# Reading a broadcast row back four steps later, and splitting the memory in the first four merged tiles

## Chip, cores and metric

The kernel runs on one core of a Trainium2 chip. The time is device microseconds of one execution. The engines are TensorE (PE, with its weight loads PEld), VectorE (DVE), ScalarE (ACT), GpSimd (POOL) and SyncE (SP), which here only issues DMAs. Each engine works through its own queue in order; engines wait for one another through semaphores.

## The reference

One layer of a hybrid decoder trunk on 512 rows of 1024 values, with 256 memory rows.

```python
h = rms_norm(x, norm_mix)
q_a, k_a, v_a, u_b, gate_b, gate_c, g_a, g_b = split(h @ w_in)
o_a = stick_breaking_attention(q_a, k_a, v_a)          # 8 heads of 64, causal
y_b = gate_b * causal_depthwise_conv(gate_c * u_b, conv_w)
merged = sigmoid(g_a) * (o_a @ w_branch_a) + sigmoid(g_b) * (y_b @ w_branch_b)
x = x + merged @ w_mix_out
m = rms_norm(mem, norm_mem_kv)                         # the memory: 256 x 1024
x = x + memory_cross_attention(rms_norm(x, norm_mem_q), m, w_mem_q, w_mem_kv, w_mem_o)
gate, up = split(rms_norm(x, norm_ffn) @ w_ffn_in)
x = x + (silu(gate) * up) @ w_ffn_out
return rms_norm(x, norm_final)
```

The attention's weight of key s for query t is sigmoid(z) times the product of (1 − sigmoid(z)) over the keys between them; it is computed as the exponential of sums of logarithms.

## The kernel before

Everything is held transposed: features on the 128 partitions, the 512 rows along the free axis, 8 tiles of 128 features. Every fp32 product is made of three matmuls on a high and a low part (names that end in `h` and `l`): ACT casts the high part, and DVE subtracts it to get the low part (`split`, L176 and L177 or L172 and L174). A weight tile is loaded by SP into `wr`, cast by ACT to `wh` (L149), and DVE makes `wl` (L150); there are four buffers of each. A projection (`project`, `gemm`) is 24 matmuls of 512 columns into one of two PSUM banks, which DVE then reads out (L294, L353, L372, L378, L387).

The first stage is a loop of 16 steps (L561), over four pairs of heads p and, for each, four blocks of 128 keys kt from 3 down to 0; step i has p = i // 4, so steps 9 and 13 are the same block kt = 2 of pairs 2 and 3. In a step PE computes the scores of the next block (`scores`, z at L445), adds the sums of logarithms to the scores of this one (`weights`, z at L488 and L491), and multiplies the weights of the block before with the values (`values`, o at L510). Projections from the list `fill` are put between them. Around the matmuls:

- `scores`: ACT and DVE make the logarithms `e`, POOL zeroes what lies above the diagonal (`causal`, L402, the select).
- `fails` (L460): ACT and DVE split `e` into `l`, which L491 multiplies in the next step.
- `weights` (L480): ACT takes the exponential `a` (L493), POOL applies the select to `a`, DVE multiplies and splits it into `ah` and `al` (L497, L498).
- `values`: after the last block of a pair, DVE adds the two halves `ot` (L519).

The memory's norm is prepared inside this loop. At steps 1, 3, 5 and 7 (`MEM_AT`) ACT squares a quarter of the memory; at step 9 (`MEAN_AT`) `mem_factors` (L536) makes the 256 factors 1/rms as `rm`, on 128 partitions x 2. POOL writes them to DRAM as one row `rmd` (L542) and reads the row back broadcast to all partitions as `rmb` (L544). `rm` scales the memory's values (`vm`, L670) and `rmb` its keys (`km`, L649), both much later.

The second stage (L618) makes the eight tiles of `merged`: two gates (a projection and its readout g, L353), two branch products br, their products and sum on DVE (L633, L634), and a split into `mh` and `ml`. After tile `SUMS_AT` = 1 POOL starts `weight_sums`, which loads pieces of the last weight matrix, adds them on POOL (`pre`, L595) and stores the sums; it goes on to the end of the stage. After tiles 0, 2, 4 and 6 `mem_split` loads two of the memory's eight feature tiles and splits them, with the gain, into `mgh` (ACT, L611) and `mgl` (DVE, L612). Those parts are read by the products `km` and `vm` that follow the stage. The loads of `mem_split` and those of the residual `x` (L705) share eight buffers (`xpool`); the parts take buffers of the pool `upool` (50 buffers), in the order in which the program asks for them.

A scheduler sets each engine's order from the program's order and the dependencies. `after(i, earlier)` (L105) adds a dependency that only orders instructions and makes nothing wait.

Of the kernel before, what the change touches and what calls it, by code (L numbers as in the profile page):

```python
# [8 lines left out]
F32 = mybir.dt.float32  # L9
# [4 lines left out]
P = 128  # L14
D = 1024
S = 512
KD = D // P
# [4 lines left out]
MEM = 256  # L22
# [6 lines left out]
EPS = 1e-6  # L29
MEM_AT = (1, 3, 5, 7)  # L30
MEAN_AT = 9
EARLY = 2
WARM = 8
FIRST = 4
# [9 lines left out]
def hybrid_layer(ctx: ExitStack, tc: tile.TileContext, xT_d, memT_d, mem_d, cols_d, wv_d, win_d,  # L44
                 wbr_d, wmix_d, wmq_d, wmk_d, wmv_d, wmo_d, wfi_d, wfo_d, gfin_d, out):
    nc = tc.nc

    cpool = ctx.enter_context(tc.tile_pool(name="cpool", bufs=1))
# [14 lines left out]
    def nm(s):  # L63
        count[0] += 1
        return f"{s}{count[0]}"

    def unit(s, cols=512):
        return upool.tile([P, cols], F32R, tag="u", name=nm(s), padded_shape=[P, 512])
# [34 lines left out]
    exps, casts, lead, lows, loads = [], [], [], [], []  # L103

    def after(i, earlier):  # L105
        for e in earlier:
            tc.add_manual_dep(i.ins, e.ins.name, mybir.DependencyInfo(
                mybir.DependencyClass.NoSync, mybir.DependencyReason.DATA), reason="order")
# [7 lines left out]
    def rstd_of(var, n, s, tables=()):  # L116

        def new(t):
            return tmp(t, n) if n > TT else spool.tile([P, n], F32, tag=t, name=nm(t))

        v, y, a = new("rv"), new("ry"), new("ra")
        r = cpool.tile([P, n], F32, tag=s, name=nm(s))
        after(nc.scalar.activation(y, var, AF.Ln, bias=eps_t), tables)
        nc.vector.tensor_scalar(out=v, in0=var, scalar1=EPS, scalar2=None, op0=ALU.add)
        exps.append(nc.scalar.activation(y, y, AF.Exp, scale=-0.5))
        nc.vector.tensor_tensor(out=a, in0=y, in1=y, op=ALU.mult)
        nc.vector.scalar_tensor_tensor(out=a, in0=a, scalar=-0.5, in1=v, op0=ALU.mult,
                                       op1=ALU.mult)
        nc.vector.scalar_tensor_tensor(out=r, in0=a, scalar=1.5, in1=y, op0=ALU.add, op1=ALU.mult)
        return r  # L130
# [171 lines left out]
    def settle_behind(*last):  # L302
        while urgent or behind:
            (urgent or behind).pop(0)(*last)
# [131 lines left out]
    def scores(p, kt):  # L436
        c0, n = span(kt)
        keys = slice(kt * P, (kt + 1) * P)
        zs[p, kt] = []
        for hs in heads_of(kt):  # L440
            bank = ztile("z")
            zs[p, kt].append(bank)
            for i, h in enumerate(hs):
                for part in range(2):
                    nc.tensor.matmul(bank[:, i * n:(i + 1) * n], ks[p][h][:, keys],  # L445
                                     qs[p][h][part][:, c0:], start=i + part == 0, stop=part == 1,
                                     skip_group_check=True)
        for hs, bank in zip(heads_of(kt), zs[p, kt]):
            w = len(hs) * n
            z = bank[:, :w]  # L450
            e = tmp("e")[:, :w]
            nc.scalar.activation(e, z, AF.Abs)
            nc.scalar.activation(e, e, AF.Exp, scale=-1.0)
            nc.scalar.activation(e, e, AF.Ln, bias=1.0)
            nc.vector.scalar_tensor_tensor(out=e, in0=z, scalar=0.0, in1=e, op0=ALU.max,
                                           op1=ALU.add)
            causal(by_head(e, n))
            urgent.append(lambda *last, e=e, hs=hs: fails(p, kt, hs, e, n, last))
# [21 lines left out]
    def weights(p, kt):  # L480
        c0, n = span(kt)
        av[p, kt] = {}
        for hs, bank in zip(heads_of(kt), zs[p, kt]):
            w = len(hs) * n
            z = bank[:, :w]
            if kt < TT - 1:
                for part in carried(p, kt, hs):
                    nc.tensor.matmul(by_head(z, n)[:, :, P:], neg1, part, start=False, stop=False,  # L488
                                     skip_group_check=True)
            for part in sp[p, kt, hs]:  # L490
                nc.tensor.matmul(z, negtri, part, start=False, stop=True, skip_group_check=True)  # L491
            a = tmp("a")[:, :w]
            exps.append(nc.scalar.activation(a, z, AF.Exp))  # L493
            causal(by_head(a, n))
            ah, al = unit("ah")[:, :w], unit("al")[:, :w]
            r = r0[:, kt:kt + 1]
            nc.vector.tensor_scalar(out=ah, in0=a, scalar1=r, scalar2=None, op0=ALU.mult)  # L497
            als.append(nc.vector.scalar_tensor_tensor(out=al, in0=a, scalar=r, in1=f(ah),  # L498
                                                      op0=ALU.mult, op1=ALU.subtract))
            for h in hs:  # L500
                av[p, kt][h] = part_of((ah, al), hs, (h,), n)
# [21 lines left out]
    def load_mem(k2, t):  # L523
        nc.sync.dma_start(t, memT_d[2 * k2 * P:(2 * k2 + 2) * P, :].rearrange("(j p) t -> p j t",
                                                                              p=P))
# [3 lines left out]
    def mem_square(i):  # L529

        h, t = divmod(i, MT)
        mk = f(unit("mk"))
        nc.sync.dma_start(mk, mem_d[t, :, h * 512:(h + 1) * 512])
        nc.scalar.activation(mk, mk, AF.Square, scale=D ** -0.5, accum_out=ms[:, i:i + 1])

    def mem_factors():  # L536

        var = spool.tile([P, MT], F32, tag="mv", name="mv", bufs=1)
        nc.vector.tensor_tensor(out=var, in0=ms[:, :MT], in1=ms[:, MT:], op=ALU.add)
        rm = rstd_of(var, MT, "rm")  # L540
        d = dpool.tile([1, MEM], F32, tag="rm", name="rmd")
        nc.gpsimd.dma_start(d.rearrange("o (t p) -> p (o t)", p=P), rm)  # L542
        rmb = cpool.tile([P, MEM], F32, tag="rmb", name="rmb")
        nc.gpsimd.dma_start(rmb, d.broadcast_to([P, MEM]))  # L544
        return rm, rmb

    fill = []
    for p in range(TT):
        if p + 1 < TT:
            fill += [(qk_part, p + 1, 0), (qk_part, p + 1, 1)]  # L550
        fill += [(conv, p, i) for i in range(3)]
    for m in range(EARLY):
        fill += [(gate, m, 0), (gate, m, 1)]
# [7 lines left out]
    for i in range(len(steps) + 1):  # L561
        if i in MEM_AT:
            mem_square(MEM_AT.index(i))
        if i == MEAN_AT:
            rm, rmb = mem_factors()
        some = []
        while fill and (i == len(steps) or len(some) < (2 if steps[i][1] == 1 else 1)):
            some.append(fill.pop(0))
        if i + 1 < len(steps):
            to = lambda: scores(*steps[i + 1])  # L570
            if len(some) == 1:
                midway.append(to)
            else:
                some.insert(len(some) // 2, (to,))
        for g, *args in some:
            g(*args)
        if i < len(steps):
            weights(*steps[i])
        if i > 0:
            values(*steps[i - 1])  # L580
        settle_behind(*exps[-1:], *joined[-1:])
# [22 lines left out]
    def mem_split(k2):  # L604
        mk = xpool.tile([P, 2, MEM], F32, tag="x", name=nm("mk"))
        load_mem(k2, mk)
        his, los = unit("mgh"), unit("mgl")
        for j in range(2):
            k = 2 * k2 + j
            hi, lo = (u[:, j * MEM:(j + 1) * MEM] for u in (his, los))  # L610
            nc.scalar.activation(hi, mk[:, j, :], AF.Copy, scale=g_kv[:, k:k + 1])  # L611
            nc.vector.scalar_tensor_tensor(out=lo, in0=mk[:, j, :], scalar=g_kv[:, k:k + 1],  # L612
                                           in1=f(hi), op0=ALU.mult, op1=ALU.subtract)
            mg.append((hi, lo))
# [3 lines left out]
    for m in range(KD):  # L618
        sig = []
        for j in range(2):  # L620
            if (m, j) not in gates:
                gate(m, j)
            t = gates.pop((m, j))
            sigmoid = nc.scalar.activation(t, t, AF.Sigmoid)
            after(sigmoid, exps[-2:])
            sig.append(t)
        w = load_w(wbr_d[m])
        for j in (1, 0):
            if m == 0 and j == 0:
                gate(EARLY, 0)  # L630
            ps = mmtile("br")
            gemm(ps, w, (oT, yb)[j], 4 * j)
            nc.vector.tensor_tensor(out=sig[j], in0=ps, in1=sig[j], op=ALU.mult)  # L633
        nc.vector.tensor_tensor(out=sig[0], in0=sig[0], in1=sig[1], op=ALU.add)  # L634
        if m < KD - 1:
            merged.append(split(sig[0], "m"))
        if m == SUMS_AT:
            weight_sums(range(SUMS_FIRST), merged[m][0])
        if m % 2 == 0:
            mem_split(m // 2)  # L640


    km = []
# [796 lines left out]
```

## Time and profile before

| what | value |
|---|---|
| median of 3 runs | 851.28 us (851.17 to 852.26) |
| profiled execution, its own time | 852.17 us |
| its span, first to last instruction | 850.3 us |
| mean granted clock of TensorE | 0.993 |
| DMA moved | 143.73 MB, mean 169 GB/s |

Where the stages lie in the profiled execution, by the rows in order of time: the 16 steps until about 199 us, the merged tiles until 308.7 us, the memory's keys until 332 us, then its values, the residual products, the attention over the memory, and the FFN with the end. The rows below are read as: start in us, length in us, engine, line, operation, tile written <- tiles read, shape, count; in brackets at the end the idle time of that engine just before, and what ended it. A row of a stretch of several instructions has their count and their total length.

### The profile page before, as it was taken

How to read it: one execution, taken by the hardware profiler on the slowest of the kernel's cores; microseconds unless marked ns; L12 is line 12 of the kernel's file. 1: busy time of each engine (PE TensorE's matmuls, PEld its weight loads, DVE VectorE, ACT ScalarE, POOL GpSimd, SP SyncE). 2: the span in 40 equal slices, each digit the busy share in tenths (PEclk: the TensorE clock that was granted, in tenths of full speed). 3: DMA queues.
4: the chain of work that ended last, by engine and by line, in shares of the span. 5: the costliest groups of instructions: out<-in, count | busy, mean ns of one | idle time of the engine just before them, and what ended most of it. 6: DMA issues, size and time to landing. Idle time of an engine off the chain costs nothing.

```text
span 850.3 us, 12669 instructions
## 1 busy us (share of the span) xinstructions
PE 837.4 (98%) x4763; PEld 737.8 (87%) x4763; DVE 657.2 (77%) x1049; ACT 459.4 (54%) x818; POOL 158.0 (19%) x165
## 2 busy tenths in 40 slices
PE   9999998999999999999999999999999999999996
PEld 7888886888888889888888889999999999988885
DVE  8869978896766686578555688888888888899886
ACT  7567866575333254534444565655555555666654
POOL 0011121210466650065000010211111110000401
PEclk9999998999999999999999999999999999999998
DMA  8453453225587765566341324776776773465552
GB/s 298 154 162 104 137 89 82 92 74 173 210 309 292 287 250 184 175 244 234 131 122 50 91 71 141 189 189 176 183 188 176 192 191 91 144 222 204 176 184 99
DMA packets 51360, 143.73 MB, mean 169 GB/s; under 512 B 5762, under 2 KB 7042, under 8 KB 48483
## 3 DMA queue, kind: packets, MB, share of 16 engines
q1 hardware_dynamic: 41650, 107.89, 38.1%
q0 software_dynamic: 9360, 34.75, 15.7%
q8 instruction: 37, 0.61, 0.3%
q10 hardware_dynamic: 288, 0.28, 0.1%
q14 instruction: 25, 0.20, 0.1%
HBM read 125.20 MB, written 13.64 MB: 163 GB/s over the span
## 4 chain that ended last, share of the span: by engine, by line
PE 93%; DVE 4%; DMA 1%; ACT 1%; issue 0%; POOL 0%; DVEq 0%; POOLq 0%
PE z L864 15%; PE p L1133 12%; PE y L864 7%; PE pr L154 6%; PE pr L155 6%; PE pr L156 6%; PE v L864 4%; PE r L155 3%; PE r L154 3%; PE r L156 3%; PE v L272 3%; PE mq L156 2%; PE mq L154 2%; PE mq L155 2%; PE br L154 2%; PE br L155 2%
## 5 line engine op out<-in xcount | busy, mean ns | idle before, releaser
L149 ACT CAST wh<-wr 128x1024 fp32r<-128x1024 f32 x84 | 88.0, 1052 | 151.3 <-issue 67.1
L150 DVE TENSOR_TENSOR wl<-wr,wh 128x1024 fp32r<-128x1024 f32 x84 | 111.1, 1325 | 38.0 <-ACT wh L149 37.8
L154 PE MATMUL pr<-xgh,wh 128*128 128x512 f32 x288 | 113.8, 395 | 0.0
L155 PE MATMUL pr<-xgl,wh 128*128 128x512 f32 x288 | 113.3, 393 | 0.0
L156 PE MATMUL pr<-xgh,wl 128*128 128x512 f32 x288 | 112.9, 392 | 0.0
L595 POOL TENSOR_TENSOR pre<-pre 128x512 f32<-128x512 f32 x44 | 72.5, 1652 | 30.1 <-DMA pre<-in_w_ffn_out_dram 27.8
L833 POOL DMA_DIRECT2D ws<-in_w_ffn_in_dram x22 | 26.6, 1209 | 255.7 <-DVE wf L854 122.8
L864 PE MATMUL z<-xdh,wf 128*128 128x256 f32 x352 | 70.4, 283 | 0.0
L156 PEld LDWEIGHTS pr<-xgh,wl 128*128 128x128 f32 x288 | 54.6, 190 | 11.8
L154 PEld LDWEIGHTS pr<-xgh,wh 128*128 128x128 f32 x288 | 54.7, 190 | 10.9
L155 PEld LDWEIGHTS pr<-xgl,wh 128*128 128x128 f32 x288 | 54.7, 190 | 10.5
L885 ACT COPY sa<-z 128x256 f32<-128x256 f32 x44 | 16.4, 373 | 80.9 <-PE z L864 80.9
L864 PEld LDWEIGHTS z<-xdh,wf 128*128 128x128 f32 x352 | 58.0, 192 | 0.0
L854 DVE TENSOR_TENSOR wf<-s,wf 128x512 fp32r<-128x512 f32 x44 | 30.4, 691 | 25.7 <-ACT wf L853 25.3
L864 PE MATMUL z<-xdl,wf 128*128 128x256 f32 x176 | 49.8, 283 | 0.0
L945 DVE TENSOR_TENSOR wl<-wr,wh 128x1024 fp32r<-128x1024 f32 x33 | 41.0, 1242 | 3.7 <-ACT wh L1012 3.6
L1012 ACT CAST wh<-wr 128x1024 fp32r<-128x1024 f32 x33 | 34.6, 1049 | 4.2 <-DMA wr<-sums 1.9
L864 PE MATMUL y<-xch,wf 128*128 128x256 f32 x176 | 35.4, 283 | 0.0
L864 PE MATMUL v<-xoh,wf 128*128 128x256 f32 x176 | 35.4, 283 | 0.0
L864 PE MATMUL z<-xf,wf 128*128 128x256 f32 x264 | 35.4, 283 | 0.0
L864 PE MATMUL z<-xch,wf 128*128 128x256 f32 x176 | 35.3, 283 | 0.0
L864 PE MATMUL y<-xoh,wf 128*128 128x256 f32 x176 | 35.3, 283 | 0.0
(348 smaller groups left out, 2399.6 us busy)
## 6 DMA issues: line engine op xcount, KB each, us to landing
wr<-in_w_in_dram SPq DMA_DIRECT2D x36, 512.0 KB, 3.4
pre<-in_w_ffn_out_dram POOLq DMA_DIRECT2D x11, 1024.0 KB, 7.7
sums<-pre POOLq DMA_DIRECT2D x11, 1024.0 KB, 5.0
ws<-in_w_ffn_in_dram SPq DMA_DIRECT2D x22, 512.0 KB, 3.7
wg<-in_w_ffn_in_dram SPq DMA_DIRECT2D x22, 512.0 KB, 4.5
ws<-in_w_ffn_in_dram POOLq DMA_DIRECT2D x22, 512.0 KB, 6.0
wr<-sums SPq DMA_DIRECT2D x22, 512.0 KB, 4.0
wr<-in_w_ffn_out_dram SPq DMA_DIRECT2D x16, 512.0 KB, 3.8
```

Source lines behind the costliest of these rows:

```text
L149: after(nc.scalar.copy(h2, raw), lead[-1:])
L150: lows.append(nc.vector.tensor_tensor(out=l2, in0=raw, in1=f(h2), op=ALU.subtract))
L154: nc.tensor.matmul(ps, a[0], b[0], start=start, stop=False, **kw)
L155: nc.tensor.matmul(ps, a[0], b[1], start=False, stop=False, **kw)
L156: nc.tensor.matmul(ps, a[1], b[0], start=False, stop=stop, **kw)
L595: nc.gpsimd.tensor_tensor(out=t[:, a, :], in0=t[:, a, :], in1=t[:, b, :], op=ALU.add)
L833: nc.gpsimd.dma_start(s13, a[:, 0:4:3, :], accum_op=ALU.add)
L854: nc.vector.tensor_tensor(out=w[:, 1, :], in0=raw, in1=f(w[:, 0, :]), op=ALU.subtract)
L864: nc.tensor.matmul(ps[:, :HS], a, b, start=i < 3 and k == 0 and j == 0, stop=k == KP - 1 and j == 2, skip_group_check=True)
L945: nc.vector.tensor_tensor(out=lo, in0=src, in1=f(hi), op=ALU.subtract)
L1012: nc.scalar.copy(hi, raw)
L1133: nc.tensor.matmul(res[i][s2], a[:, ts], b, start=j == 0 and n == 0, stop=n == 2 and j == (BEHIND - 1 if (i, s2) == (5, 1) else NJ - 1))
```

## The change

It has two parts. The read-back of the row is taken out of `mem_factors`, which now returns the DRAM row, and is issued at step 13 (`ROW_AT`), ordered behind the last exponential that was issued by then, that of step 12. And `mem_split` is called after the merged tiles 0, 1, 2 and 3 in place of 0, 2, 4 and 6.

```diff
+ROW_AT = 13
...
-        rmb = cpool.tile([P, MEM], F32, tag="rmb", name="rmb")
-        nc.gpsimd.dma_start(rmb, d.broadcast_to([P, MEM]))
-        return rm, rmb
+        return rm, d
...
         if i == MEAN_AT:
-            rm, rmb = mem_factors()
+            rm, rmd = mem_factors()
+        if i == ROW_AT:
+            rmb = cpool.tile([P, MEM], F32, tag="rmb", name="rmb")
+            after(nc.gpsimd.dma_start(rmb, rmd.broadcast_to([P, MEM])), exps[-1:])
...
-        if m % 2 == 0:
-            mem_split(m // 2)
+        if m < KD // 2:
+            mem_split(m)
```

In the rows that follow, the number behind a name tells its buffers apart, and the lines of the changed kernel are one to three higher.

POOL around step 9, before: `a_1336` is the `a` of step 8's weights, `e_1314` the `e` of step 9.

```order
L402 AFFINE_SELECT a_1263<-a_1263 128x128
L542 DMA rmd<-rm_1380 128x2x1
L402 AFFINE_SELECT e_1314<-e_1314 128x2x128
L544 DMA rmb<-rmd 128x256
L402 AFFINE_SELECT a_1336<-a_1336 128x256
L402 AFFINE_SELECT a_1446<-a_1446 128x2x128
```

The same place in the changed kernel:

```order
L403 AFFINE_SELECT a_1263<-a_1263 128x128
L543 DMA rmd<-rm_1380 128x2x1
L403 AFFINE_SELECT e_1314<-e_1314 128x2x128
L403 AFFINE_SELECT a_1336<-a_1336 128x256
L403 AFFINE_SELECT a_1444<-a_1444 128x2x128
```

The select of `a_1336` now follows that of `e_1314` at once; the write `rmd` has kept its place. Four steps later POOL has, in the changed kernel (`a_1727` is the `a` of step 12, `e_1702` the `e` of step 13):

```order
L403 AFFINE_SELECT a_1663<-a_1663 128x128
L403 AFFINE_SELECT e_1702<-e_1702 128x2x128
L567 DMA rmb<-rmd 128x256
L403 AFFINE_SELECT a_1727<-a_1727 128x256
L403 AFFINE_SELECT a_1819<-a_1819 128x2x128
```

Before, these four selects stood there without the read between them. The other engines' order in the 16 steps is the same in both kernels.

DVE in merged tiles 6 and 7, before: `ml_2788` is the low part of merged tile 6, `mgl_2794` the memory's last parts, `g_2830` and `g_2864` the gates of tile 7.

```order
L150 TENSOR_TENSOR wl_2905<-wr_2902,wh_2904 128x1024
L353 TENSOR_TENSOR g_2830<-pr_2805,r0b_363 128x512
L150 TENSOR_TENSOR wl_2946<-wr_2943,wh_2945 128x1024
L174 TENSOR_TENSOR ml_2788<-g_2715,mh_2787 128x512
L612 SCALAR_TENSOR_TENSOR mgl_2794<-mk_2791,gcol,mgh_2793 128x256 x2
L353 TENSOR_TENSOR g_2864<-pr_2839,r0b_363 128x512
L150 TENSOR_TENSOR wl_2981<-wr_2978,wh_2980 128x1024
```

And in the changed kernel, where `ml_2689` is the low part of merged tile 5 and `ml_2796` that of tile 6:

```order
L151 TENSOR_TENSOR wl_2905<-wr_2902,wh_2904 128x1024
L354 TENSOR_TENSOR g_2830<-pr_2805,r0b_363 128x512
L151 TENSOR_TENSOR wl_2946<-wr_2943,wh_2945 128x1024
L175 TENSOR_TENSOR ml_2689<-g_2616,mh_2688 128x512
L175 TENSOR_TENSOR ml_2796<-g_2723,mh_2795 128x512
L354 TENSOR_TENSOR g_2864<-pr_2839,r0b_363 128x512
L151 TENSOR_TENSOR wl_2981<-wr_2978,wh_2980 128x1024
```

The two splits `mgl` are gone from this place, and tile 5's `ml`, which stood ahead of tile 6's gates before, stands here. The memory's parts have taken two buffers earlier, and tile 5's parts now get buffers that PE has to free first: its cast `mh` waits for PE, which it did not before. ACT's casts are moved in the same way.

DVE after merged tile 3, in the changed kernel (`ml_2467` is the low part of tile 3; `g_2509` is the next tile's first gate):

```order
L636 TENSOR_TENSOR g_2394<-g_2394,g_2428 128x512
L151 TENSOR_TENSOR wl_2588<-wr_2585,wh_2587 128x1024
L175 TENSOR_TENSOR ml_2467<-g_2394,mh_2466 128x512
L614 SCALAR_TENSOR_TENSOR mgl_2473<-mk_2470,gcol,mgh_2472 128x256 x2
L354 TENSOR_TENSOR g_2509<-pr_2484,r0b_363 128x512
L151 TENSOR_TENSOR wl_2622<-wr_2619,wh_2621 128x1024
```

Before, `ml` was followed there by the gate's readout at once; the same holds for tile 1. PE's order is the same in both kernels. On SP the loads of `x` for the residual's tiles 5 to 7, which need the buffers of the memory's tiles, move ahead with the splits, and one weight load goes behind the third memory load.

## The prediction

> **What bounds the kernel now.** I read the page first, then TensorE's waits, then order of time around the one long wait.
>
> ```profile
> PE 837.4 (98%) x4763; PEld 737.8 (87%) x4763; DVE 657.2 (77%) x1049; ACT 459.4 (54%) x818; POOL 158.0 (19%) x165
> PEclk9999998999999999999999999999999999999998
> PE z L491 <- DVE l L417: 4.0, 1, 4.0
> PE br L154 <- DVE g L353: 0.4, 1, 0.4
> ```
>
> TensorE (PE) is busy for 837.4 of 850.3 us, so it is the bound nearly everywhere, and a change pays only where PE stands still or runs slowly. The waits (total us, times, longest) leave two such places inside the kernel: one of 4.0 us, one of 0.4 us. The clock row (40 slices of 21.3 us) has an 8 in the seventh slice, 127.5 to 148.8 us, and one in the last.
>
> ```profile
> 128.51 0.39 PE L491 MATMUL z<-l,negtri 128*128 128x512 f32 x1
> 132.92 0.79 PE L491 MATMUL z<-l,negtri 128*128 128x512 f32 x1 [4.03 <-DVE l L417]
> 134.26 0.73 PE L154 MATMUL pr<-xgh,wh 128*128 128x512 f32 x1
> 139.30 0.40 PE L154 MATMUL pr<-xgh,wh 128*128 128x512 f32 x1
> 171.28 0.62 PE L491 MATMUL z<-l,negtri 128*128 128x512 f32 x2
> 172.13 0.44 PE L154 MATMUL pr<-xgh,wh 128*128 128x512 f32 x1
> 174.94 0.39 PE L154 MATMUL pr<-xgh,wh 128*128 128x512 f32 x1
> 128.51:132.92 4.41, 0.39 (x3) 0.07 (x2) 2.75 (x6) 0.74 (x2) 0.99 (x2) 0.92 0.60 142
> 132.92:139.30 6.38, 6.38 (x17) 5.18 (x18) 5.76 (x11) 5.89 (x12) 1.25 (x3) 0.52 0.28 64
> ```
>
> These are PE's rows in order of time in step 9 (first four) and step 13 (next three), and two rows of windows (length, then busy time of PE, PEld, DVE, ACT, POOL, the granted clock, DMA). Steps 9 and 13 are the same stretch of code for head pairs 2 and 3: two `z` matmuls of line 491, four short ones, then projections `pr`. In step 9 the second L491 waits 4.03 us, and the clock granted afterwards is 0.52 until 139.30. From the first L491 to the 13th `pr` matmul (both ends shown) step 9 takes 139.30 − 128.51 = 10.79 us, step 13 takes 174.94 − 171.28 = 3.66 us, at full clock without a wait. So this place loses **7.13 us**: 4.03 of waiting, and 3.10 because the matmuls behind it run at half clock.
>
> ```profile
> 119.72 0.73 POOL L542 DMA_DIRECT2D rmd<-rm  x1 [3.62 <-DVE rm L129]
> 121.07 0.40 POOL L402 TENSOR_SCALAR_AFFINE_SELECT e<-e 128x256 f32<-128x256 f32 x1 [0.62 <-DVE e L455]
> 129.04 0.57 POOL L544 DMA_DIRECT2D rmb<-rmd  x1 [7.57 <-DMA rmd<-rm]
> 129.63 0.42 POOL L402 TENSOR_SCALAR_AFFINE_SELECT a<-a 128x256 f32<-128x256 f32 x1
> 121.81 0.39 ACT L493 ACTIVATE a<-z 128x256 f32<-128x256 f32 x1
> 121.95 1.23 DVE L150 TENSOR_TENSOR wl<-wr,wh 128x1024 fp32r<-128x1024 f32 x1 [0.17 <-ACT wh L149]
> 130.08 0.35 DVE L497 TENSOR_SCALAR ah<-a,r 128x256 fp32r<-128x256 f32 x1 [6.91 <-POOL a L402]
> 132.17 0.69 DVE L417 TENSOR_TENSOR l<-e,l 128x512 fp32r<-128x512 f32 x1
> ```
>
> Who made `l` late: POOL's read-back `rmb` stands in its queue ahead of the select of `a`, and waits 7.57 us for the write of `rmd` to land. `a` was ready at 121.81 + 0.39 = 122.20, but its select starts at 129.63. DVE is in order: `ah` waits for the select, and behind `ah` are queued `ot`, `al`, `ot` and then `l`, for which PE waits.
>
> **The change, first part: the read moves four steps on.** Nothing is added or removed; one DMA issue moves past 12 POOL instructions. Without it the select runs at 122.2 to 122.7; DVE is at `wl` until 121.95 + 1.23 = 123.18, so `ah` starts at 123.2 instead of 130.08, 6.88 us earlier. With the same sequence behind it, `l` ends at 132.86 − 6.88 = 126.0; PE wants it one matmul (0.23) after 128.51, at 128.74. So the whole wait goes, with 2.7 us to spare. Step 13 has the same margin in the trace:
>
> ```profile
> 165.03 0.51 POOL L402 TENSOR_SCALAR_AFFINE_SELECT a<-a 128x256 f32<-128x256 f32 x1 [0.73 <-ACT a L493]
> 166.54 0.34 DVE L497 TENSOR_SCALAR ah<-a,r 128x256 fp32r<-128x256 f32 x1
> 168.63 0.69 DVE L417 TENSOR_TENSOR l<-e,l 128x512 fp32r<-128x512 f32 x1
> 139.78 1.21 DVE L150 TENSOR_TENSOR wl<-wr,wh 128x1024 fp32r<-128x1024 f32 x1
> 143.39 0.39 PE L156 MATMUL pr<-xgh,wl 128*128 128x512 f32 x1
> 134.00:200.00 66.00, 66.00 (x301) 55.48 (x301) 58.08 (x95) 45.99 (x83) 11.13 (x21) 0.96 0.30 99
> rmd<-rm POOLq DMA_DIRECT2D x1, 1.0 KB, 9.0
> rmb<-rmd POOLq DMA_DIRECT2D x1, 128.0 KB, 4.1
> L649 DVE TENSOR_TENSOR km<-km,rmb x8: 420/426/426, 311.8 to 331.9; 128x256 f32<-128x256 f32 x8
> ```
>
> There `l` ends at 168.63 + 0.69 = 169.32. The second L491 of the pair shown at 171.28 (0.62 for two, 0.39 for one) starts 0.23 later, at 171.51: 2.2 us of margin. The moved read now stands just ahead of this select of `a`, where POOL sits idle for 0.73 us; its issue took 0.57, so I price it at 0. At its worst it is as long as the longest select of this kernel, 1.8 us, and makes `a` 1.1 us late; but `a` ends 1.0 us before DVE comes to it, and behind that lie the 2.2 us. PE waits only if POOL is held for over 0.73 + 1.0 + 2.2, about 4 us. The write, issued at 119.72, landed 9.04 later at 128.76; the read now comes at about 164.3 − 7.1 = 157.2, 28 us after it, so the only wait that the read has is over. Its own 4.1 us are hidden, since `rmb` is first used at 311.8.
>
> What is late next, with the wait gone? DVE comes 6.88 us earlier, PE 7.13, so PE gets 0.25 us closer to DVE. The nearest product it uses is `wl`, which ends at 140.99 and is first used at 143.39: 2.40 us, still 2.15. SP's queue needs `qk` results that DVE and ACT now make about 7 us earlier.
>
> The clock row in that window counts as a term of its own. The Trainium skill, "TensorE: Matmul & The Clock Gate", section "What's actually happening", says that an idle window of about 3.4 us halves the clock and that such windows run on freely, whatever the kernel does. By that rule a pause of 4.03 us need not close the gate in every execution, and the gain would then be the wait alone. The trace agrees in this execution (0.52 after the pause); that it holds in the timed ones no row shows.
>
> Value taken for the first part: 7.13 us (ends: 4.03, no clock loss in the timed runs, and 7.13; nothing in the step is lost beyond what step 13 lacks).
>
> **Second part: the memory's splits after the first four merged tiles.** Four pairs of ACT copies `mgh` and four pairs of DVE splits `mgl` stay; those of m=4 and m=6 move to m=1 and m=3. Their loads stay at 192 to 195 us (row below), but for one weight load that goes behind the third of them, 0.45 us. Because two more buffers are taken early, the split `ml` of merged tile 5 slides behind tile 7's first gate.
>
> ```profile
> L524 SPq DMA_DIRECT2D mk<-in_memT_dram x4: 378/452/1029, 192.3 to 194.8; - x4
> 300.12 1.77 DVE L174 TENSOR_TENSOR ml<-g,mh 128x512 fp32r<-128x512 f32 x1
> 301.82 3.37 DVE L612 SCALAR_TENSOR_TENSOR mgl<-mk,gcol,mgh 128x256 fp32r<-128x256 f32 x2
> 305.11 0.68 DVE L353 TENSOR_TENSOR g<-pr,r0b 128x512 f32<-128x512 f32 x1
> 305.84 0.50 PE L154 MATMUL br<-oh,wh 128*128 128x512 f32 x1 [0.37 <-DVE g L353]
> 213.38 0.87 DVE L612 SCALAR_TENSOR_TENSOR mgl<-mk,gcol,mgh 128x256 fp32r<-128x256 f32 x2
> 221.19 0.69 DVE L353 TENSOR_TENSOR g<-pr,r0b 128x512 f32<-128x512 f32 x1 [2.29 <-PE pr L156]
> 248.39 0.69 DVE L353 TENSOR_TENSOR g<-pr,r0b 128x512 f32<-128x512 f32 x1 [2.29 <-PE pr L156]
> 248.21 1.05 ACT L149 CAST wh<-wr 128x1024 fp32r<-128x1024 f32 x1 [3.18 <-PE pr L155]
> 250.54 0.33 SPq L141 DMA_DIRECT2D wr<-in_w_branch_dram  x1
> ```
>
> At the end of the stage `ml` and two `mgl` took 1.77 + 3.37 = 5.14 us ahead of `g`; now two `ml` stand there, 2 × 1.77 = 3.54 at the same slow pace. `g` comes 1.6 us earlier and PE's 0.37 us go. More can't be won here: PE waits nowhere else in this stage. At m=1 and m=3 DVE idles 2.29 us before the next `g`, and the undisturbed pair costs 0.87; ACT idles 3.18 us (m=3), and its pair is 0.9. So 0. Its other end: if POOL's additions run at that moment, the pair is 3.37 us and `ml` 1.77, the load that cost 0.37 at 305; twice, 0.74. The fourth late load of `x` now waits on SP for m=3's split, ahead of the weights issued at 250.54. That split ends 0.87 into the idle time that begins at 248.39 − 2.29, so at 247.0: 3.5 us of room. I take −0.37, with ends −0.37 and +0.37.
>
> **Sum.** Against the profiled execution's 852.17 us (span 850.3, 1.87 around it): 852.17 − 7.13 − 0.37 = **844.67**. The median of the runs shown is 851.28, 0.89 lower; the same 7.50 off it gives 843.78. The highest run, 852.26, equals the profiled one, so profiling as such adds little. I take 844.5, nearer to the sum in which every term was seen; 0.2% is 1.7 us, about what a measurement can tell from no change.
>
> **Rivals.**
>
> - The clock doesn't fall in the timed runs, so only 4.03 + 0.37 = 4.40 is won: 851.28 − 4.40 = 846.9. For it: one trace shows one execution. Against it: a run without the half clock would be 3.10 under the profiled 852.17, at 849.1, and the lowest is 851.17. This is what the free-running window in the Trainium skill, "TensorE: Matmul & The Clock Gate", section "What's actually happening", would do. Chance 0.10.
> - DVE becomes what PE waits for. DVE is busy 58.08 of the 66 us behind the place, so it can't follow much faster; if it eats the 3.10 that the full clock gives, 852.17 − 4.40 = 847.8. Against it: 2.15 us of margin at the nearest use, and step 13 runs at full clock with the same load. Chance 0.09.
> - The wait re-forms with nothing won, because the select of `a` was held by something else besides the read. `a` was ready at 122.20 and POOL idle from 121.47, so there is no sign of it: 850.9 to 851.3. Chance 0.04.
> - Slower: the read holds POOL in step 13. If its issue had to wait for a transfer as long as the write's 9.0 us plus its own 4.1, POOL would be held 13.7 us, less the idle 0.73 and the 3.2 us of margin: PE waits 9.7 us, and with 3.10 for the clock the time is 844.7 + 12.8 = 857.5. It decides from 4 us on (PE waits) and makes the kernel slower than before by over 0.2% from about 10 us. Against it: its one wait is for a write 28 us old. Chance 0.03.
>
> **How the numbers follow.** The forecast has 0.74, with a range of its own of 843.3 (median less 7.50, and half a microsecond of spread) to 846.0 (the profiled sum, 0.74 if both new places collide, and as much spread). The range for 8 in 10 reaches on to the two middle rivals, 847.8. Faster by over 0.2%: 0.74 + 0.10 + 0.09 = 0.93; within 0.2%: 0.04; slower: 0.03.
>
> **What would show it.** Right: no wait of PE on L491 near 129 us; clock 9 in the seventh slice; the `ah` of 130.08 near 123.2; `rmb` issued near 157 us (164.3 less 7) between two selects and the `a` behind it not late; no wait of `br` on `g`. The gaps of PE sum to about 7 us less, and the span is near 842.8. Wrong: a PE wait of over 0.5 us between 126 and 200, a half clock that stays, DVE splits at m=1 or m=3 of over 2 us followed by a PE wait, or a weight load on SP delayed behind an `x` load.

## The result, and the profile after

| | before | changed |
|---|---|---|
| median of 6 runs | 851.75 us (851.17 to 852.47) | 844.59 us (844.14 to 844.98) |
| span of the profiled execution | 850.3 us | 842.4 us |
| mean granted clock of TensorE | 0.993 | 0.998 |

The changed kernel takes 0.9915 of the time before, with a 95% interval of 0.9902 to 0.9928: 7.16 us less. The page of the changed kernel, with the busy times and the clock row (40 slices, now of 21.1 us):

```profile
PE 833.9 (99%) x4763; PEld 735.5 (87%) x4763; DVE 653.5 (78%) x1049; ACT 459.0 (54%) x818; POOL 152.8 (18%) x165
PEclk9999999999999999999999999999999999999999
```

The 8 in the seventh slice is gone, and PE's busy time falls by 3.5 us although it has as many matmuls: the slow ones ran at half clock. PE's waits in the changed kernel, the whole answer (us in total, times, longest):

```profile
PE warm L233 <- DVE neg L92: 1.4, 1, 1.4
```

Only the wait at the very start is left. The rows of the changed kernel in order of time around step 9 (its lines are one to three higher than before):

```profile
119.67 0.73 POOL L543 DMA_DIRECT2D rmd<-rm  x1 [3.62 <-DVE rm L130]
122.21 1.18 POOL L403 TENSOR_SCALAR_AFFINE_SELECT a<-a 128x256 f32<-128x256 f32 x1 [0.78 <-ACT a L494]
123.42 0.35 DVE L498 TENSOR_SCALAR ah<-a,r 128x256 fp32r<-128x256 f32 x1 [0.30 <-POOL a L403]
125.52 0.69 DVE L418 TENSOR_TENSOR l<-e,l 128x512 fp32r<-128x512 f32 x1
128.46 0.62 PE L492 MATMUL z<-l,negtri 128*128 128x512 f32 x2
132.12 0.39 PE L155 MATMUL pr<-xgh,wh 128*128 128x512 f32 x1
```

The write of the row is issued as before, but the select of `a` behind it no longer waits; `ah` starts at 123.42 in place of 130.08. `l` ends at 126.21, PE wants it at 128.46 + 0.23 = 128.69, so the two L492 run as one piece. The last row is the 13th `pr`: the stretch that took 10.79 us takes 132.12 − 128.46 = 3.66, to the hundredth what step 13 took before.

A better measure of a stage than the span is the distance between two matmuls of PE, since it leaves out the start of the kernel, which varies by about a microsecond. For step 9 I take the first `z` of the next two blocks' scores. Before:

```profile
124.80 0.87 PE L445 MATMUL z<-qk,qk 128*128 128x384 f32 x4
142.03 1.07 PE L445 MATMUL z<-qk,qk 128*128 128x512 f32 x4
```

And after:

```profile
124.76 0.87 PE L446 MATMUL z<-qk,qk 128*128 128x384 f32 x4
134.84 1.07 PE L446 MATMUL z<-qk,qk 128*128 128x512 f32 x4
```

That is 142.03 − 124.80 = 17.23 before and 10.08 after, 7.15 us. The same for other stretches, in every kernel that was profiled (each one execution):

| kernel | step 9 | step 11 | step 13 | first br to first km |
|---|---|---|---|---|
| before | 17.23 | 7.93 | 10.08 | 109.46 |
| before, second execution | 16.92 | 7.93 | 10.09 | 108.80 |
| changed | 10.08 | 7.92 | 10.08 | 108.80 |
| read alone | 10.08 | 7.93 | 10.08 | 108.82 |
| splits alone | 17.28 | 7.92 | 10.08 | 108.80 |
| read one select later | 10.08 | 7.93 | 10.08 | 108.80 |
| write and read in step 13 | 10.08 | 7.92 | 15.85 | 108.80 |
| POOL held in step 13 | 10.08 | 7.93 | 10.09 | 108.80 |
| fill with 17 | 14.51 | 9.55 | 10.08 | 108.82 |
| fill with 17, order held | 14.41 | 9.42 | 10.08 | 109.56 |
| fill with 13 | 14.31 | 9.54 | 10.08 | 108.80 |
| fill with 9 | 15.97 | 7.93 | 10.08 | 108.80 |
| fill with 4 | 17.24 | 7.93 | 10.09 | 108.80 |

(Step 9, 11 and 13: from the first `z` of the scores of steps 10, 12 and 14 to that of the next step; us.) The table answers most of what follows: a number away from its column's usual one is a place where PE stood still or ran slowly.

### The profile page after: what moved, and what is told of

The parts are those of the page before. It is cut to its first block, busy times and chain, and to the rows that moved or that the text cites. A ratio compares the mean times of both kernels' runs of the same rounds, so it can differ in the third digit from the quotient of the medians.

```text
span 842.4 us, 12670 instructions
## 1 busy us (share of the span) xinstructions
PE 833.9 (99%) x4763; PEld 735.5 (87%) x4763; DVE 653.5 (78%) x1049; ACT 459.0 (54%) x818; POOL 152.8 (18%) x165
## 4 chain that ended last, share of the span: by engine, by line
PE 99%; DVE 0%; ACT 0%; DVEq 0%; issue 0%
PE z L866 15%; PE p L1135 12%; PE pr L155 8%; PE pr L156 8%; PE pr L157 8%; PE y L866 8%; PE v L866 4%; PE r L156 3%; PE r L155 3%; PE r L157 3%; PE v L273 3%; PE mq L157 2%; PE mq L155 2%; PE mq L156 2%; PE br L157 2%; PE br L156 2%
```

## Experiments

### The two parts alone

Theory A is the prediction's: the read's wait costs 7.13 us, the splits 0.37, apart from each other. First the read alone, the splits as before:

```diff
-        if m < KD // 2:
-            mem_split(m)
+        if m % 2 == 0:
+            mem_split(m // 2)
```

> The kernel before with only the read of the row moved to step 13; the memory's splits stay at merged tiles 0, 2, 4 and 6. Theory A (the read's wait costs 7.13 us, the splits 0.37, independent of each other): 7.13 us under the kernel before, so about 844.6 beside 851.75, PE's wait on L491 gone, its 0.37 us wait of br on g still there. Rival B (the two parts help each other, or the splits carry more of the gain than the trace of before shows): 846 or more.

Measured: 844.40 us beside 850.90, ratio 0.9922 (0.9908 to 0.9935). That is the whole gain of the change, within the intervals (6.50 us here and not 7.13, which is taken up under "Span and time"). But PE's wait of `br` on `g`, which theory A left in place, is gone too. The read alone, DVE in order of time at the end of the merged stage:

```profile
290.84 1.23 DVE L151 TENSOR_TENSOR wl<-wr,wh 128x1024 fp32r<-128x1024 f32 x1 [0.21 <-ACT wh L150]
291.99 1.78 DVE L175 TENSOR_TENSOR ml<-g,mh 128x512 fp32r<-128x512 f32 x1
293.69 3.37 DVE L614 SCALAR_TENSOR_TENSOR mgl<-mk,gcol,mgh 128x256 fp32r<-128x256 f32 x2
296.98 0.68 DVE L354 TENSOR_TENSOR g<-pr,r0b 128x512 f32<-128x512 f32 x1
```

And the same `wl` in the kernel before:

```profile
298.25 1.94 DVE L150 TENSOR_TENSOR wl<-wr,wh 128x1024 fp32r<-128x1024 f32 x1 [0.21 <-ACT wh L149]
```

`ml` and the two `mgl` take as long as before, so the difference isn't in them. The `wl` ahead of them took 1.94 before and 1.23 here. That 0.71 decides, since PE waited 0.37 there.

Then the splits alone, on the kernel before:

```diff
-        if m % 2 == 0:
-            mem_split(m // 2)
+        if m < KD // 2:
+            mem_split(m)
```

> The kernel before with only the memory's splits moved to merged tiles 0 to 3; the read stays in step 9. Theory A: 0.37 us under the kernel before, about 851.4, within what a timing can tell from no change; PE's wait on L491 of 4.0 us and the half clock behind it stay, br's wait on g goes. Rival B: 850 or less.

Measured: 851.21 us beside 850.90, ratio 1.0000 (0.9991 to 1.0009). Its waits of PE show the 4.0 us, and no `br`:

```profile
PE z L491 <- DVE l L417: 4.0, 1, 4.0
PE warm L232 <- DVE neg L91: 1.4, 1, 1.4
```

So the splits alone gain nothing that a timing can tell. A second execution of the kernel before says why:

> The kernel before, unchanged, in a second profiled execution. If PE's 0.37 us wait of br on g at the end of the merged stage belongs to the kernel's order, it is there again and the stage from the first br to the first km takes 109.46 us again; if it was an accident of that one execution, the stage takes 108.80, as in the fill with 4, and the second part of the change has nothing to win. PE's wait of 4.0 us on L491 stays; the half clock behind it lasts 6.8 us if its length is fixed, 3.4 or 6.8 if it goes in whole windows that start anywhere.

Measured in this one run: 850.99 us, a wait of 3.84 us on L491, and 6.83 us of half clock behind it. In it `wl` and its neighbours read as follows:

```profile
297.62 1.23 DVE L150 TENSOR_TENSOR wl<-wr,wh 128x1024 fp32r<-128x1024 f32 x1 [0.21 <-ACT wh L149]
300.47 3.38 DVE L612 SCALAR_TENSOR_TENSOR mgl<-mk,gcol,mgh 128x256 fp32r<-128x256 f32 x2
```

`wl` takes 1.23, and PE doesn't wait for `g`: the merged stage takes 108.80, with the splits at their old place. Over all thirteen executions this `wl` took 1.22 to 2.17 us. Of the eight with the splits at the old place, the two in which it took 1.94 and 2.05 have the wait (109.46 and 109.56 in the table), and the six with 1.23 to 1.62 don't. With the new place there is no wait in five, not even where `wl` took the longest. The kernel of the next section (its splits at the new place), DVE and PE:

```profile
291.65 2.17 DVE L151 TENSOR_TENSOR wl<-wr,wh 128x1024 fp32r<-128x1024 f32 x1 [0.21 <-ACT wh L150]
297.14 0.68 DVE L354 TENSOR_TENSOR g<-pr,r0b 128x512 f32<-128x512 f32 x1
298.70 0.39 PE L155 MATMUL br<-oh,wh 128*128 128x512 f32 x1
```

`g` ends 0.88 ahead of `br` here, although `wl` took 0.94 longer than in the read alone, where `g` ends at 297.66 for a `br` at 297.90, 0.24 ahead. So the second part gives `g` 0.88 + 0.94 − 0.24 = 1.58 us more room, and takes away a wait that comes in some executions and costs about 0.7 us when it comes. Where it comes, the merged stage loses more than the 0.37 us that the wait is listed with: 109.46 − 108.80 = 0.66.

### Does the distance count, or only the one select?

The read is put back to step 9, one POOL instruction behind its old place:

```diff
-ROW_AT = 13
+ROW_AT = 9
...
-            causal(by_head(a, n))
+            selects.append(causal(by_head(a, n)))
...
-            after(nc.gpsimd.dma_start(rmb, rmd.broadcast_to([P, MEM])), exps[-1:])
+            after(nc.gpsimd.dma_start(rmb, rmd.broadcast_to([P, MEM])), selects[-1:])
```

> The changed kernel with the read put back to step 9, but behind the select of a instead of ahead of it: one POOL instruction later, not four steps. Theory A (only the select held behind the read mattered): POOL waits for the write until about 128.7 as before, but the next select is due only at 130.58, so nothing is late: 844.6, no PE wait on L491. Rival C (any wait of POOL in step 9 is passed on, or distance in steps is what counts): a PE wait again, 848 to 851.5.

Measured: 844.95 us beside 850.90, ratio 0.9924 (0.9912 to 0.9937). POOL's rows in order of time:

```profile
122.80 1.17 POOL L403 TENSOR_SCALAR_AFFINE_SELECT a<-a 128x256 f32<-128x256 f32 x1 [0.79 <-ACT a L494]
129.70 0.57 POOL L567 DMA_DIRECT2D rmb<-rmd  x1 [5.73 <-DMA rmd<-rm]
131.17 0.40 POOL L403 TENSOR_SCALAR_AFFINE_SELECT a<-a 128x256 f32<-128x256 f32 x1 [0.91 <-DVE e L456]
```

POOL still waits 5.73 us for the write, and nobody is late: the next select comes 0.91 after the read was issued, and waits for DVE. A wait costs what stands behind it in the queue. One place would have been enough; it leaves 0.91 us of room, where four steps leave the write 28 us.

### The stall put into step 13

The write, too, is taken out of step 9; write and read stand together ahead of step 12's select of `a`:

```diff
-        nc.gpsimd.dma_start(d.rearrange("o (t p) -> p (o t)", p=P), rm)
         return rm, d
...
-            causal(by_head(a, n))
+            for rm, rmd in (row,) if row else ():
+                after(nc.gpsimd.dma_start(rmd.rearrange("o (t p) -> p (o t)", p=P), rm), exps[-1:])
+                read = nc.gpsimd.dma_start(rmb, rmd.broadcast_to([P, MEM]))
+            after(causal(by_head(a, n)), (read,) if row else ())
```

> The changed kernel with the write also moved: write and read stand together in step 13 between the select of e and that of a. Theory A (the wait of a read for a fresh write holds POOL wherever it stands): the write issued near 157.2 lands 9.0 us later, the select of a ends near 167.3 in place of 158.35, DVE's ah is 8.0 late, l 8.0 late, less 2.2 us of margin: PE waits 5.8 us, and 3.1 more for the half clock, 853.4. Rival C (step 9 was special, for instance by the squares and loads of the memory): 844.6. Rival D (the half clock does not follow every pause): about 850.3.

Measured: 850.41 us beside 850.90, ratio 0.9995 (0.9987 to 1.0004): the gain is given back. Rows of POOL, DVE and PE in order of time, and two windows on both sides of the granted clock's step (last but two of their columns):

```profile
157.41 0.73 POOL L496 DMA_DIRECT2D rmd<-rm  x1
160.82 0.69 DVE L418 TENSOR_TENSOR l<-e,l 128x512 fp32r<-128x512 f32 x1
166.81 0.57 POOL L497 DMA_DIRECT2D rmb<-rmd  x1 [8.67 <-DMA rmd<-rm]
167.84 0.35 DVE L501 TENSOR_SCALAR ah<-a,r 128x256 fp32r<-128x256 f32 x1 [6.33 <-POOL a L403]
168.34 0.30 PE L514 MATMUL o<-ah,v 128*128 128x128 f32 x1 [3.38 <-DVE ah L501]
169.80:173.40 3.60, 3.60 (x11) 2.80 (x10) 3.51 (x7) 3.58 (x8) 0.74 (x1) 0.53 0.20 32
173.40:173.80 0.40, 0.40 (x4) 0.31 (x3) 0.40 (x2) 0.40 (x2) 0.00 (x0) 1.00 0.00 0
```

The stall moved with the pair: nothing about step 9 was special. Its price is 15.85 − 10.08 = 5.77, not the 5.8 + 3.1 = 8.9 expected, for two reasons. The scheduler put `l` ahead of `ah` on DVE, so PE had its L492 in time and waited for the values instead, 3.38 and 0.34 us; and the half clock behind it lasted 3.6 us at most, about half of the 6.4 us and more of step 9 before. The time is that of rival D, 850.3, but not for D's reason, since the clock did fall.

### How long may POOL be held?

Ten selects of a spare tile ahead of step 12's select of `a`, in the changed kernel:

```diff
+            held = []
+            for _ in range(10 if (p, kt) == (3, 3) else 0):
+                held.append(nc.gpsimd.affine_select(out=spare, in_=spare, compare_op=ALU.is_ge,
+                                                    fill=0.0, base=0, pattern=[[-1, P]],
+                                                    channel_multiplier=1))
+                after(held[-1], exps[-1:])
-            causal(by_head(a, n))
+            after(causal(by_head(a, n)), held[-1:])
```

> The changed kernel with ten selects of a spare tile 128x128 on POOL ahead of step 12's select of a (in step 13), about 2.9 us of work, so that POOL is held about 3.5 us with the read. Theory A (PE waits only if POOL is held over about 4 us): no change, 844.6, no PE wait on L491 in step 13. Rival E (step 13 has less room than the rows say, for instance as DVE slows beside POOL's work): a PE wait, 845.5 to 849 with a half clock.

Measured: 844.66 us beside 851.33, ratio 0.9922 (0.9908 to 0.9935), so as fast as the change. The rows:

```profile
158.10 4.11 POOL L499 TENSOR_SCALAR_AFFINE_SELECT spare<-spare 128x128 f32<-128x128 f32 x9
162.16 0.41 POOL L405 TENSOR_SCALAR_AFFINE_SELECT a<-a 128x256 f32<-128x256 f32 x1
162.87 0.69 DVE L420 TENSOR_TENSOR l<-e,l 128x512 fp32r<-128x512 f32 x1
164.31 0.62 PE L494 MATMUL z<-l,negtri 128*128 128x512 f32 x2
```

The selects took 0.46 each, not the 0.29 that I had counted with, so POOL was held from 157.28 to 162.16, 4.88 us; `l` ends at 163.56 and is wanted at 164.54. In this kernel step 13 thus has more room than the 4 us of the prediction. But some of it comes from the scheduler, which put two `ot` ahead of `ah` and `l` ahead of `al`. The changed kernel's own order was not tried: there `l` ends 161.43 + 0.69 − 159.35 = 2.77 us after `ah` starts, so with `ah` at 162.61 as here it would, as an estimate, have ended at 165.38, 0.8 too late, as the 4 us would have it.

### Is the half clock a loss of its own?

The prediction took 7.13 apart into a wait of 4.03 and 3.10 of half clock. Here PE works through the wait of the kernel before on matmuls that add zero (`zero` is a tile of zeros), so the stall upstream stays and the clock doesn't fall:

```diff
-            for part in sp[p, kt, hs]:
+            for j, part in enumerate(sp[p, kt, hs]):
+                if j == 1 and (p, kt) == (2, 2):
+                    for _ in range(17):
+                        nc.tensor.matmul(z, zero, sp[p, kt, hs][0], start=False, stop=False,
+                                         skip_group_check=True)
```

> The kernel before, with 17 matmuls of zeros times the high part of l, accumulated into the same bank (they add nothing), between the two L491 of step 9, so that PE works through its 4.03 us wait (17 x 0.23 = 3.9 us). Theory A (3.10 us of the loss are the half clock, and the pause causes it): PE runs on at full clock behind it, 3.1 us under the kernel before, about 848.65. Rival D (the half clock has another cause, or its loss is made up later): no change, 851.75.

Measured: 851.27 us beside 851.33, ratio 0.9996 (0.9988 to 1.0005). Nothing is gained, though the clock never falls. The table shows where it went: step 9 takes 14.51 in place of 17.23, 2.72 less, and step 11 takes 9.55 in place of 7.93, 1.62 more. Step 10, which isn't in the table, takes another 0.31 more (10.79 in place of 10.48). The 0.79 us that are left lie within the interval, which reaches to a gain of 1.0. The added matmuls had also made the scheduler change DVE's order behind them, so the run was repeated with two constraints on ACT that hold DVE's order:

```diff
+                pinned.append(exps[-1])
+                after(lns[-1], pinned)
...
-        after(nc.scalar.copy(h2, raw), lead[-1:])
+        after(nc.scalar.copy(h2, raw), pinned if len(lows) == 18 else lead[-1:])
```

> The fill with 17 matmuls, with two order constraints on ACT (a weight cast and a logarithm behind the exponential of step 9), so that DVE's order up to step 11's l stays nearly that of the kernel before. From the first qk z to the first km the kernel before takes 183.2 us (without the br wait). If the half clock is a loss of its own: 3.1 less, 180.1. If the late DVE stands behind it: the rows of before leave step 11's second l 2.1 us of margin, so of 3.1 won 1.0 and a restart are given back as a wait on l: 181.3 to 181.9. If all of it is eaten: 182.5 or more, as in the first fill.

Measured: 850.64 us beside 850.99, ratio 0.9993 (0.9984 to 1.0002). A gain of 3.1 us would be a ratio of 0.9964, and is excluded. Rows of this kernel, PE in steps 9 and 11 and DVE in step 11:

```profile
132.70 0.50 PE L500 MATMUL z<-l,negtri 128*128 128x512 f32 x1 [0.23 <-DVE l L422]
153.57 0.50 PE L500 MATMUL z<-l,negtri 128*128 128x512 f32 x1 [0.42 <-DVE l L422]
154.29 0.68 DVE L422 TENSOR_TENSOR l<-e,l 128x512 fp32r<-128x512 f32 x1
155.03 0.50 PE L500 MATMUL z<-l,negtri 128*128 128x512 f32 x1 [0.56 <-DVE l L422]
```

Step 9 is 2.82 us shorter than before, and step 11 is 1.49 longer (9.42 − 7.93), of which 0.42 and 0.56 are listed as waits for `l`. So about half of what step 9 won is lost again two steps later, most of it as waits for DVE. From the first `z` of step 9's stretch to the first `km`, without the wait of `br`, this kernel takes 181.9 us, which is the outcome expected where the late DVE stands behind it. (In this execution the wait of `br` on `g` came too: 109.56.) DVE was made late by the same stall; while PE ran at half clock, DVE could come nearer. So the half clock was partly cover, and is a loss of its own only for the part that isn't given back. The change doesn't meet this, since it brings DVE forward together with PE.

Fewer matmuls leave a longer pause, which shows what pause closes the clock gate, that is, halves the granted clock:

```diff
-                    for _ in range(17):
+                    for _ in range(9):
```

> As the fill with 17, with 9 such matmuls: 2.1 us of the wait are filled, a pause of about 2.0 us is left. Theory A, where a pause has to be about as long as the 3.4 us windows: 848.65, full clock. If shorter pauses close the gate too: 850.5 to 851.75.

Measured: 850.00 us beside 851.33, ratio 0.9983 (0.9974 to 0.9992). Step 9 takes 15.97, 1.26 less than before, step 11 stays at 7.93, and the time shows a gain: here nothing is given back. The time lies between the two that were expected. In the profiled execution the clock falls, for half as long as before; by the mean clocks of the runs it can have fallen in four of the eleven at most (0.995 to 0.997, 850.82 us in the mean), while the seven others have 0.998 or 0.999, as kernels without a pause have (849.67 us). The wait, and windows of the slow stretch and of what follows:

```profile
133.71 0.75 PE L499 MATMUL z<-l,negtri 128*128 128x512 f32 x1 [2.00 <-DVE l L421]
133.60:137.20 3.60, 3.49 (x10) 2.96 (x11) 3.50 (x7) 3.53 (x8) 0.00 (x0) 0.53 0.34 78
137.20:137.60 0.40, 0.40 (x3) 0.32 (x2) 0.37 (x2) 0.40 (x2) 0.00 (x0) 0.99 0.01 0
```

With 4 matmuls:

> As the fill with 17, with 4 such matmuls: 0.9 us filled, a pause of about 3.1 us is left. Theory A, where only a whole idle window closes the gate: 848.65; if the pause of 3.1 us suffices: 851.75.

Measured: 851.34 us beside 851.33, ratio 1.0002 (0.9993 to 1.0011). The wait is 2.92 us, and the clock falls for twice as long:

```profile
132.60:139.60 7.00, 6.61 (x18) 5.37 (x19) 6.42 (x11) 6.27 (x13) 1.01 (x3) 0.51 0.27 64
139.60:140.00 0.40, 0.40 (x3) 0.32 (x2) 0.40 (x2) 0.06 (x1) 0.30 (x1) 1.00 0.65 92
```

With 13:

> As the fill with 17, with 13 matmuls: 3.0 us filled, a pause of about 1.2 us is left. If a pause of 1.2 us still closes the gate: a half clock of 3.4 us behind it; if not: full clock.

Measured: a wait of 1.04 us, and full clock behind it (the window until 142); one run, 850.24 us. Step 11 gives back 1.61 (9.54 − 7.93), as in the fill with 17.

```profile
132.58 0.50 PE L499 MATMUL z<-l,negtri 128*128 128x512 f32 x1 [1.04 <-DVE l L421]
134.00:142.00 8.00, 8.00 (x37) 6.59 (x37) 6.70 (x12) 5.32 (x12) 0.95 (x3) 1.00 0.41 115
```

## Why the prediction came out right, point by point

**The read.** Predicted 7.13 us, measured 7.15 from `z` to `z` (17.23 − 10.08), and the read alone gives the whole gain. The chain was as told: POOL's read, the select behind it, `ah`, `l`, PE. `ah` was forecast for 123.2 and came at 123.42, because the select took 1.18 in place of 0.42; `l` ended at 126.21 for 126.0, with 2.5 us of the 2.7 to spare.

**The new place.** Forecast for about 157.2, and at no cost. POOL, and then DVE, in the changed kernel:

```profile
157.16 0.57 POOL L567 DMA_DIRECT2D rmb<-rmd  x1
157.85 0.50 POOL L403 TENSOR_SCALAR_AFFINE_SELECT a<-a 128x256 f32<-128x256 f32 x1
159.35 0.34 DVE L498 TENSOR_SCALAR ah<-a,r 128x256 fp32r<-128x256 f32 x1
```

The read is issued without a wait, and `ah` starts 1.0 us after its select has ended, as in step 13 before. The slower rival needed POOL held for over 4 us; the stall put into step 13 shows that it works where the write is fresh, at a lower price than I gave it, and it doesn't arise where the write is old.

**What is late next.** DVE came 0.25 us nearer, as said, in step 11: the second `l` there was 2.11 us early before (153.94 + 0.68 against 156.73) and is 1.86 early now:

```profile
147.00 0.68 DVE L418 TENSOR_TENSOR l<-e,l 128x512 fp32r<-128x512 f32 x1
149.31 0.63 PE L492 MATMUL z<-l,negtri 128*128 128x512 f32 x2
133.12 1.21 DVE L151 TENSOR_TENSOR wl<-wr,wh 128x1024 fp32r<-128x1024 f32 x1
136.20 0.39 PE L157 MATMUL pr<-xgh,wl 128*128 128x512 f32 x1
```

The nearest use of `wl` has 136.20 − 134.33 = 1.87 us, not 2.15: this `wl` came 6.66 earlier, not 6.88.

**The clock.** The rival in which the clock doesn't fall in the timed runs is out. The whole gain was seen in them, the three executions with a wait of 3.8 to 4.0 us each have a half clock of 6.83 us, and the mean clock is on record for 63 other runs of the kernel before: 42 have 0.993 or 0.994, as those three do, and none has the 0.998 of the changed kernel. When it falls, and for how long, the clock records of the traces show. In all thirteen the granted clock changes only on a grid of 3.413 us that isn't tied to the kernel: the first rise to full clock comes 4.64 to 7.50 us after the first instruction, and the half clock of step 9 begins 126.29 us, 37 steps of the grid, after that rise in all five executions that have one (that of step 13 after 163.84, 48 steps). The kernel before, from one edge of the grid to the next and to the third (PE's busy time is the second number behind the bounds, the granted clock the last but two):

```profile
128.82:132.23 3.41, 0.07 (x1) 0.00 (x0) 2.09 (x5) 0.05 (x1) 0.99 (x2) 1.00 0.66 154
132.23:139.06 6.83, 6.14 (x16) 4.98 (x17) 6.18 (x11) 6.58 (x13) 1.01 (x3) 0.50 0.30 74
```

The clock fell behind every such window in which PE stood idle for 2.00 us or more, and behind none with 1.61 or less. It rose again after one window where PE worked all through it (the fill with 9, and the stall in step 13), and after two where the pause reached 0.31 to 0.91 us into the first. By these figures a pause of 3 us can fall on the grid in two halves and cost no clock at all; one of 4.03 can't, since at least 2.01 of it lies in one window.

By the rule of the Trainium skill ("TensorE: Matmul & The Clock Gate", "What's actually happening"), an idle window of about 3.4 us is needed and windows run freely, so a pause of 4.03 would often have left the clock alone. The traces agree with the length of a window and with its running freely, but not with a whole idle one: waits of 2.00 and 2.92 us closed the gate, 1.04 didn't.

**The step that failed** is the second part's term: "`g` comes 1.6 us earlier and PE's 0.37 us go", counted at −0.37 on top of the read. It was read off one execution, in which a `wl` ran 0.71 us longer than in others, and it is absent in the second execution of the kernel before. That `g` comes 1.6 us earlier was right (1.58); that PE has a use for it was not, in most executions. The read alone gives 844.40 beside 844.95 and 844.59 of kernels with both parts, so the second part shows no gain in the time. The total hardly shows it, since 0.37 is less than the runs spread. The other end of this term, +0.37 or more if the early splits met POOL's additions, didn't come either: the pairs at m=1 and m=3 took 0.87 us each, and DVE still idled 1.50 us behind them.

**A step that was right as a sum and wrong as a price**: "4.03 of waiting, and 3.10 because the matmuls behind it run at half clock". Both went, but the rivals treated the 3.10 as something that could be won or lost by itself; with the stall left upstream and the pause filled, about half of what was won is given back to DVE in step 11. The runs of the kernel before say the same: the 15 of the 63 with a mean clock of 0.996 or 0.997 took 850.81 us in the mean, the 42 with 0.993 or 0.994 took 851.40. That is at least one window of half clock less (3.41 us of it lower the mean by 0.002), so 1.7 us of PE's work, and it is worth 0.6 us.

**Span and time.** The spans differ by 7.9 us and the medians by 7.16 (6.50 and 6.67 in the comparisons of the read alone and of the held POOL). Of the 7.9, 0.66 is the wait of `br` that doesn't come in every execution, and 0.31 is that step 9 took 16.92 in the second execution of the kernel before, with a wait of 3.84 us, and 17.23 in the profiled one, with 4.03. That second execution has a span of 849.1, 6.7 above 842.4.

**How close the number came is luck.** The forecast was 844.5, and 844.59 was measured. Its sum starts from the profiled execution's 852.17, which is 0.91 above the median of all 69 runs of the kernel before (851.26). It takes 7.50 off, where the 20 runs of the four kernels with the read out of the way have a median of 844.61: 6.65 less. The two errors, 0.91 and 0.85, cancel. That the place, the chain and some 7 us of PE's time were right is not luck.

## What to carry to other kernels

A DMA read issued on POOL's queue behind the write that it reads stopped POOL until the write had landed (waits of 5.73 to 8.67 us), and the cost is whatever stands behind it: look for a place in the same queue where the next instruction is due later than the landing, and one instruction may be enough (here it was). Behind a pause of PE of 2 us or more look for a half clock, and take both away together by making the late operand early; where the pause was only filled, so that the clock stayed up, half or more of what was won came back as waits at the next places where the late engine was needed (the fills with 17 and 13; in the profiled execution of the fill with 9 nothing came back, but only 1.26 us had been won). A term of a few tenths read from one execution is worth a second execution before it is given a price.

## What was not expected of the hardware

- A half clock came in one or two windows of 3.41 us, and the length of the pause alone doesn't order them: two after waits of 2.92, 3.84, 3.99 and 4.03 us, one after 2.00 and one after 3.38, none after 1.04 (each one execution). The place of the pause on the grid does.
- DVE's `wl` of 128x1024 behind tile 7's first gate took 1.22 to 2.17 us in thirteen executions, in the same place of DVE's order. Its length goes with POOL's additions: where the next of them started 0.07 to 0.21 us after `wl`, it took 1.22 or 1.23 (six executions); where it started 0.54 to 1.17 us after, `wl` ended 1.00 us behind that start (six; the one between, 0.30, took 1.43). How the two hinder each other is not shown.
- The write of 256 factors, 1.0 KB, took 8.8 to 9.2 us to land, and the read of 128 KB that follows it 3.2 to 5.5.
- The spread of the runs shrank with the stall, from 1.30 us to 0.84 (six runs each). The half clock's varying length has a part in it, 0.6 us between the runs of the kernel before with more and with less of it.
